# The end of a transformer block: last columns in two products, gate products in the gate's buffer, a quarter of the last x on TensorE

## The chip, the cores and the metric

The kernel runs on one core of one Trainium2 chip. The metric is the device time of one execution in microseconds (us), the median of three runs. A profiled execution, taken separately, gives the trace that is read below; its times are counted from the start of its span.

## The reference

One layer of a hybrid encoder block on an input x of 256 rows by 2048 columns, in float32. Three residual steps follow each other: a gated feed-forward network, a token-mixing step (chunked attention and a spatial gating unit side by side), and a second feed-forward network. Only the end of the third step matters here:

```python
h = modulate(rms_norm(x, ffn2_pre_g[l]), sh3, sc3)
y = swiglu(h, ffn2_w_gu[l], ffn2_w_down[l])
x = x + 0.5 * gt3 * rms_norm(y, ffn2_post_g[l])
```

`y` is 256 x 2048. `rms_norm` divides each row by the root of its mean square and multiplies by a gain for each column. So the last step needs, for each row, the sum of the squares of all 2048 columns of `y` before a single column of the output can be formed.

## The kernel before

The 256 rows are two tiles of 128 partitions, `t` = 0 and 1. The 2048 output columns are four blocks of `CH` = 512, `n` = 0 to 3. All big products are made of three float32r products each (helper `mm3`, lines 135 to 137): both operands are split into a high and a low part, and high*high, high*low and low*high are added in PSUM. Operands are loaded, split by ScalarE and VectorE (line 178 and 179), and multiplied by TensorE.

The feed-forward function `ffn` walks over the 5504 hidden columns in 11 chunks; the last chunk has 384. Its down projection ends in `down_last`, which adds the last chunk's contribution for all 2048 columns, and in the second feed-forward network (where `ahead` is None, so `tail` is true) this is the end of the program:

- `mm(t, n)`: 9 products of 128 x 512 into one PSUM bank (three 128-row pieces of the chunk, three products each).
- `evac(t, n, ps)`: VectorE adds the bank to `y[t]` (line 600), ScalarE squares the block and sums it (helper `square`, line 194), and VectorE multiplies the block by the gate in place (line 326). `g[0]` is the gate, one row of 2048 spread over the 128 partitions; it holds 0.5 * gt3 * ffn2_post_g. After n = 3, `rstd` (lines 199 and 201) has VectorE add the partial sums into `ms` and GpSimd raise the result to the power -1/2: that is `r`, one number for each row.
- `finish(t, y, r)`, here `finish3`: for each block j, VectorE computes x = y * r + x (line 1204), and SyncE starts the transfer of that block, 256 KB, to the output (line 1205).

The blocks of t = 0 are evacuated as their products end; the products of t = 1 follow at once, and are evacuated behind them (`late`). The program is written in this order, but a scheduler in the tile framework sets each engine's order, under `tc.high_priority()`. Tiles are taken from pools in turn: `pmm` has 6 PSUM banks, `sm` holds small tiles, and the tags "xn" and "h32" name buffers of `sm` that earlier stages use too. `new_sums(tag, n)` returns a tile for n partial sums and one column with epsilon, which GpSimd sets.

Of the kernel before, what the change touches and what calls it, by code (L numbers as in the profile page):

```python
# [12 lines left out]
F32 = mybir.dt.float32  # L13
F32R = mybir.dt.float32r
AF = mybir.ActivationFunctionType
ALU = mybir.AluOpType
AX = mybir.AxisListType

P = 128
D = 2048  # L20
# [8 lines left out]
CH = 512  # L29
# [54 lines left out]
def block_kernel(ctx: ExitStack, tc: tile.TileContext, a: dict, out: bass.AP):  # L84
    nc = tc.nc
# [8 lines left out]
    sm = ctx.enter_context(tc.tile_pool(name="sm", bufs=4))  # L94
    pmm = ctx.enter_context(tc.tile_pool(name="pmm", bufs=6, space=PSUM))
# [4 lines left out]
    def nm(s):  # L100
        uid[0] += 1
        return f"{s}_{uid[0]}"
# [30 lines left out]
    def mm3(ps, st, mv, start, stop):  # L133
        (ah, al), (wh, wl) = st, mv
        nc.tensor.matmul(ps, ah, wh, start=start, stop=False)  # L135
        nc.tensor.matmul(ps, ah, wl, start=False, stop=False)  # L136
        nc.tensor.matmul(ps, al, wh, start=False, stop=stop)  # L137
# [10 lines left out]
    def after(inst, first):  # L148

        tc.add_manual_dep(inst.ins, first.ins.name, mybir.DependencyInfo(  # L150
            mybir.DependencyClass.NoSync, mybir.DependencyReason.DATA), reason="order")
# [35 lines left out]
    def new_sums(tag, n):  # L187

        sums = sm.tile([P, n + 1], F32, tag=tag, name=nm(tag), bufs=2)
        nc.gpsimd.memset(sums[:, n:n + 1], EPS)  # L190
        return sums

    def square(junk, v, sums, i, width):
        return nc.scalar.activation(junk, v, AF.Square, scale=width ** -0.5, accum_out=sums[:, i:i + 1])
# [134 lines left out]
    def new_ysq():  # L329
        return [new_sums("ysq", 4) for _ in range(NT)]  # L330
# [16 lines left out]
    def ffn(wgu, wdn, h, avp, ahp, plan, rate, gate_of, finish, lead=(), after_lead=(), ahead=None,  # L347
# [5 lines left out]
        ps_of, acc, act_of, stat = {}, {}, {}, {}  # L353
# [222 lines left out]
        def down_last(c, g):  # L576

            off, w = CHUNKS[c]
            nk = w // P
            ysq = new_ysq()  # L580
            blocks = []
            tail = ahead is None
            for i in range(nk):
                raw = load(wdn, D * off + i * P * 2048, 2048)
                tick()
                for q in range(2):
                    wh, wl = split(raw[:, q * 1024:(q + 1) * 1024])
                    blocks += [(wh[:, :CH], wl[:, :CH]), (wh[:, CH:], wl[:, CH:])]
            if not tail:
                ahead()  # L590

            def mm(t, n):
                ps = pmm.tile([P, CH], F32, tag="mm", name=nm("dn"))
                for k in range(nk):
                    mm3(ps, (stat[c][t][0][:, k, :], stat[c][t][1][:, k, :]), blocks[n * nk + k], k == 0, k == nk - 1)
                return ps

            def evac(t, n, ps):
                ns = slice(n * CH, (n + 1) * CH)
                nc.vector.tensor_tensor(y[t][:, ns], y[t][:, ns], ps, op=ALU.add)  # L600
                return y_done(t, n, y, ysq, g, avp.tile([P, CH], F32, tag="av", name=nm("junk"), bufs=2))

            with tc.high_priority():
                for n in range(4):
                    r = evac(0, n, mm(0, n))
                late = [mm(1, n) for n in range(4)]
                if not tail:
                    finish(0, y, r)
                for n in range(4):
                    r1 = evac(1, n, late[n])  # L610
                if tail:
                    finish(0, y, r)
                finish(1, y, r1)

        todo, ready = [], []
        if plan:
# [561 lines left out]
    with ExitStack() as ahs:  # L1178
        avp = ahs.enter_context(tc.tile_pool(name="av2", bufs=2))
        gp = ahs.enter_context(tc.tile_pool(name="gp3", bufs=1))  # L1180
        prs = ExitStack()
        pre3 = prs.enter_context(tc.tile_pool(name="pre3", bufs=2))
        ahp = Lazy(tc, ahs, "ah2", 2, prs.close)
        use_slots((wx3, 3), (pre3, 2), (adap, 2), (wsp, 4))
        raw = sp3[2][0]
        lead = [sl for _, sls in sp3 for sl in sls] + [split(raw[:, 1024:])]

        def sum_tiles(t):

            flush_ada(GT[2])  # L1190
            pools = (((xp, "x0"), (xp, "x1")), ((const, "c_bc"), (gp, "gate")))[t]
            return [p.tile([P, KT, P], F32R, tag=tag, name=nm("ahl")) for p, tag in pools]

        x3 = []

        def gate3():
            flush_ada(GT[2])
            x3.extend(load_x(x2_dram, nc.gpsimd))
            return gate(2, 0.5, gp)

        def finish3(t, y, r):
            for j in range(4):
                js = slice(j * CH, (j + 1) * CH)
                nc.vector.scalar_tensor_tensor(out=x3[t][:, js], in0=y[t][:, js], scalar=r, in1=x3[t][:, js], op0=ALU.mult, op1=ALU.add)
                nc.sync.dma_start(out[t * P:(t + 1) * P, js], x3[t][:, js])

        ffn(a["w_gu2"], a["w_dn2"], h3, avp, ahp, None, 0.77, gate3, finish3, lead=lead,
            after_lead=((wx3, 3), (wsp, 4)), fast=FAST, sum_tiles=sum_tiles)

# [79 lines left out]
```

## Time and profile before

| | |
|---|---|
| median of 3 runs | 1825.6 us (1825.59 to 1826.73) |
| profiled execution, its own time | 1825.13 us |
| its span, first to last instruction | 1823.4 us |
| granted TensorE clock, mean | 0.996 |
| TensorE busy with products | 1789.1 us, 98% of the span |
| VectorE busy | 1455.0 us, 80% |
| ScalarE busy | 902.0 us, 49% |
| GpSimd busy | 33.5 us, 2% |

The span is shorter than the execution's own time by 1.73 us, which lie around it. PE is TensorE, PEld its loads of the stationary operand, DVE VectorE, ACT ScalarE, POOL GpSimd, SP SyncE; a q behind the name is the engine's queue or sequencer. A row of the chain of waits gives a start, a length and what was going on; a row of the timeline gives a start, the length of one or several instructions, the engine, the line and the tiles. A row of a table by windows gives the busy time of each engine in that stretch, the clock that TensorE was granted, the mean busy share of the 16 DMA engines and the rate in GB/s. Engines overlap one instruction's end with the next one's start, so the distance between starts can be less than the length of one.

### The profile page before, as it was taken

What the parts mean: (1) busy time and instruction counts of PE and PEld (TensorE: products, weight loads), DVE (VectorE), ACT (ScalarE), POOL (GpSimd) and SP (SyncE); (2) the same over time, 40 slices, a digit from 0 to 9 for tenths busy, and PEclk for the clock granted to TensorE, in tenths of its full rate; (3) what the DMA queues carried; (4) which work ended last, traced back from release to release, by engine and by line L of the source; (5) the groups of instructions that cost most, each with busy time, mean ns of one, the idle gap of its engine ahead of it and who ended that gap; (6) DMA issues with size and microseconds to landing.
All of it is one profiled execution on the core that took longest, in us unless ns stands there. A gap on an engine that the chain in (4) does not pass through costs nothing.

```text
span 1823.4 us, 21523 instructions
## 1 busy us (share of the span) xinstructions
PE 1789.1 (98%) x8199; PEld 1487.7 (82%) x8199; DVE 1455.0 (80%) x1659; ACT 902.0 (49%) x1166; POOL 33.5 (2%) x63
## 2 busy tenths in 40 slices
PE   7999999999999999999999999999999999999997
PEld 6777788888888898788888887888888888888886
DVE  6989997988778876858789987787447788788766
ACT  6544355444343335745555557445445455565552
POOL 0000000000000000000001100000000000000000
PEclk9999999999999999999999999999999999999999
DMA  9988788898888886469788985876556676676771
GB/s 394 390 329 315 284 320 344 328 366 332 337 327 330 319 331 240 182 242 361 286 333 329 348 349 203 317 300 250 196 188 231 214 285 240 222 266 247 257 254 69
DMA packets 75511, 522.19 MB, mean 286 GB/s; under 512 B 8416, under 2 KB 8592, under 8 KB 16656
## 3 DMA queue, kind: packets, MB, share of 16 engines
q1 hardware_dynamic: 74016, 511.36, 74.3%
q0 software_dynamic: 1296, 9.44, 1.2%
q8 instruction: 64, 1.05, 0.2%
q14 instruction: 39, 0.32, 0.1%
q10 hardware_dynamic: 96, 0.02, 0.0%
HBM read 514.47 MB, written 6.32 MB: 286 GB/s over the span
## 4 chain that ended last, share of the span: by engine, by line
PE 92%; DVE 3%; issue 3%; ACT 1%; DMA 0%; POOL 0%; POOLq 0%; DVEq 0%; SPq 0%; ACTq 0%
PE gu L137 14%; PE gu L136 14%; PE gu L135 14%; PE dn L135 8%; PE dn L136 8%; PE dn L137 8%; PE pj L135 4%; PE pj L137 4%; PE pj L136 4%; PE m L137 2%; PE m L136 2%; PE m L135 2%; PE wo L135 1%; PE wo L137 1%; PE wo L136 1%
## 5 line engine op out<-in xcount | busy, mean ns | idle before, releaser
L178 ACT CAST hi<-raw 128x1024 fp32r<-128x1024 f32 (+2 forms) x676 | 685.3, 1028 | 743.2 <-PE gu L137 301.9
L179 DVE TENSOR_TENSOR lo<-raw,hi 128x1024 fp32r<-128x1024 f32 (+2 forms) x676 | 788.1, 1190 | 205.5 <-ACT hi L178 202.5
L135 PE MATMUL gu<-hi,hhi 128*128 128x512 f32 (+1 forms) x1204 | 461.9, 387 | 8.8 <-DVE acc L417 4.2
L136 PE MATMUL gu<-lo,hhi 128*128 128x512 f32 (+1 forms) x1204 | 463.4, 385 | 0.4 <-DVE lo L179 0.3
L137 PE MATMUL gu<-hi,hlo 128*128 128x512 f32 (+1 forms) x1204 | 463.3, 385 | 0.0
L225 DVE CUSTOM_DVE_ANT_0 ada<-ada,c_bc,small 128x2048 f32<-128x2048 f32 x144 | 337.6, 2346 | 10.2 <-PE qkt L939 9.0
L135 PEld LDWEIGHTS gu<-hi,hhi 128*128 128x128 f32 x1204 | 226.1, 188 | 54.9 <-ACT hi L178 5.2
L136 PEld LDWEIGHTS gu<-lo,hhi 128*128 128x128 f32 x1204 | 227.1, 189 | 43.3 <-DVE lo L179 1.2
L137 PEld LDWEIGHTS gu<-hi,hlo 128*128 128x128 f32 x1204 | 226.9, 188 | 42.6
L135 PE MATMUL dn<-hi,ah 128*128 128x512 f32 x640 | 249.2, 389 | 0.0
L136 PE MATMUL dn<-lo,ah 128*128 128x512 f32 x640 | 249.1, 389 | 0.0
L137 PE MATMUL dn<-hi,al 128*128 128x512 f32 x640 | 249.1, 389 | 0.0
L135 PEld LDWEIGHTS dn<-hi,ah 128*128 128x128 f32 x640 | 120.1, 188 | 25.3
L136 PEld LDWEIGHTS dn<-lo,ah 128*128 128x128 f32 x640 | 120.1, 188 | 25.2
L137 PEld LDWEIGHTS dn<-hi,al 128*128 128x128 f32 x640 | 120.1, 188 | 25.0
L135 PE MATMUL pj<-hi,hhi 128*128 128x512 f32 x304 | 120.8, 397 | 0.0
L136 PE MATMUL pj<-lo,hhi 128*128 128x512 f32 x304 | 120.5, 396 | 0.0
L137 PE MATMUL pj<-hi,hlo 128*128 128x512 f32 x304 | 120.0, 395 | 0.0
L474 DVE TENSOR_TENSOR raw<-raw 128x512 f32<-128x512 f32 x96 | 66.2, 690 | 33.7 <-DMA raw<-in_w_gu_dram 32.4
L137 PEld LDWEIGHTS pj<-hi,hlo 128*128 128x128 f32 x304 | 57.1, 188 | 11.1
L135 PEld LDWEIGHTS pj<-hi,hhi 128*128 128x128 f32 x304 | 57.4, 189 | 10.6
L136 PEld LDWEIGHTS pj<-lo,hhi 128*128 128x128 f32 x304 | 57.4, 189 | 10.6
(199 smaller groups left out, 1450.3 us busy)
## 6 DMA issues: line engine op xcount, KB each, us to landing
raw<-in_w_gu_dram SPq DMA_DIRECT2D x158, 1024.0 KB, 4.9
ada<-in_w_ada_dram SPq DMA_DIRECT2D x144, 1024.0 KB, 6.9
raw<-in_w_dn_dram SPq DMA_DIRECT2D x86, 1024.0 KB, 5.0
raw<-in_w_in_dram SPq DMA_DIRECT2D x40, 1024.0 KB, 6.2
raw<-in_w_gu_dram SPq DMA_DIRECT2D x40, 768.0 KB, 4.8
raw<-in_w_out_dram SPq DMA_DIRECT2D x16, 1024.0 KB, 7.4
x<-x POOLq DMA_DIRECT2D x6, 1024.0 KB, 7.5
x<-in_x_dram SPq DMA_DIRECT2D x4, 1024.0 KB, 7.5
```

Of the source, the lines that this page charges most:

```text
L135: nc.tensor.matmul(ps, ah, wh, start=start, stop=False)
L136: nc.tensor.matmul(ps, ah, wl, start=False, stop=False)
L137: nc.tensor.matmul(ps, al, wh, start=False, stop=stop)
L178: i_hi = nc.scalar.copy(hi[:, :n], raw)
L179: i_lo = nc.vector.tensor_tensor(lo[:, :n], raw, hi[:, :n].bitcast(F32), op=ALU.subtract)
L225: inst = nc.vector.tensor_tensor_reduce(out=st, in0=st, in1=c_bc, scale=1.0, scalar=bada[:, i:i + 1], op0=ALU.mult, op1=ALU.add, accum_out ...
L474: nc.vector.tensor_tensor(blk[i], blk[i], blk[j], op=ALU.add)
```

## The change

In the tail of the second feed-forward network, for t = 1 alone:

1. The last 512 columns (n = 3) are computed as two products of 256 columns, each into a bank of its own, and are evacuated as two halves. There are then five partial sums of squares instead of four (a tile with the tag "ysq5").
2. The product with the gate is written over the gate, `g[0]`, instead of over `y[1]`. An explicit order puts the first half's gate product behind the second half's evacuation.
3. `finish3` for t = 1 forms the block j = 0 elsewhere: TensorE adds x (a product with the identity) and y * r (a product with a diagonal matrix `dg` of r, which ScalarE makes) in one PSUM bank, ScalarE copies the bank to a tile `xo` and starts its transfer from its own queue. VectorE forms the blocks 1 to 3 as before.

```diff
@@ down_last
             off, w = CHUNKS[c]
             nk = w // P
-            ysq = new_ysq()
+            tail = ahead is None
+            ysq = [new_sums("ysq", 4), new_sums("ysq5", 5) if tail else new_sums("ysq", 4)]
             blocks = []
-            tail = ahead is None
...
-            def mm(t, n):
-                ps = pmm.tile([P, CH], F32, tag="mm", name=nm("dn"))
+            def mm(t, n, cols=slice(0, CH)):
+                ps = pmm.tile([P, CH], F32, tag="mm", name=nm("dn"))[:, :cols.stop - cols.start]
                 for k in range(nk):
-                    mm3(ps, (stat[c][t][0][:, k, :], stat[c][t][1][:, k, :]), blocks[n * nk + k], k == 0, k == nk - 1)
+                    mm3(ps, (stat[c][t][0][:, k, :], stat[c][t][1][:, k, :]),
+                        [v[:, cols] for v in blocks[n * nk + k]], k == 0, k == nk - 1)
                 return ps
+
+            def evac_tail(late):
+
+                last = None
+                for i, (a, b, ps) in enumerate(late):
+                    inst = nc.vector.tensor_tensor(y[1][:, a:b], y[1][:, a:b], ps, op=ALU.add)
+                    if last:
+                        after(last, inst)
+                    square(avp.tile([P, CH], F32, tag="av", name=nm("junk"), bufs=2)[:, :b - a], y[1][:, a:b], ysq[1], i, D)
+                    prod = nc.vector.tensor_tensor(g[0][:, a:b], y[1][:, a:b], g[0][:, a:b], op=ALU.mult)
+                    last = prod if i == 3 else None
+                return rstd(ysq[1])
...
             with tc.high_priority():
                 for n in range(4):
                     r = evac(0, n, mm(0, n))
-                late = [mm(1, n) for n in range(4)]
-                if not tail:
+                if tail:
+                    hc = CH // 2
+                    late = [(n * CH, (n + 1) * CH, mm(1, n)) for n in range(3)]
+                    late += [(a, a + hc, mm(1, 3, slice(a - 3 * CH, a - 3 * CH + hc))) for a in (3 * CH, 3 * CH + hc)]
+                    r1 = evac_tail(late)
                     finish(0, y, r)
-                for n in range(4):
-                    r1 = evac(1, n, late[n])
-                if tail:
+                    finish(1, {1: g[0]}, r1)
+                else:
+                    late = [mm(1, n) for n in range(4)]
                     finish(0, y, r)
-                finish(1, y, r1)
+                    for n in range(4):
+                        r1 = evac(1, n, late[n])
+                    finish(1, y, r1)
@@ finish3
         def finish3(t, y, r):
-            for j in range(4):
+            if t:
+
+                js = slice(0, CH)
+                ps = pmm.tile([P, CH], F32, tag="mm", name=nm("xo"))
+                nc.tensor.matmul(ps, ident, x3[t][:, js], start=True, stop=False)
+                dg = sm.tile([P, P], F32, tag="h32", name=nm("dg"), bufs=2)
+                nc.scalar.mul(dg, ident, r)
+                nc.tensor.matmul(ps, dg, y[t][:, js], start=False, stop=True)
+                xo = sm.tile([P, CH], F32, tag="xn", name=nm("xo"), bufs=2)
+                nc.scalar.copy(xo, ps)
+                nc.scalar.dma_start(out[t * P:(t + 1) * P, js], xo)
+            for j in range(t, 4):
                 js = slice(j * CH, (j + 1) * CH)
```

The order of the instructions on the engines, apart from line numbers, is the same in both programs up to the last block of t = 1; a GpSimd instruction that sets one column of a sums tile also stands earlier, at the start of the program.

VectorE at the program's end, before. The tiles: `y_1872` and `x_2629` belong to t = 0, `y_1873` and `x_2630` to t = 1, `dn_14038`, `dn_14048` and `dn_14058` are the banks of t = 1 for n = 1, 2 and 3, `r_14025` and `r_14085` are r of t = 0 and 1:

```order
L600 TENSOR_TENSOR y_1873_9725<-y_1873_9725,dn_14038 128x512
L1204 SCALAR_TENSOR_TENSOR x_2629_13616<-y_1872_9724,r_14025,x_2629_13616 128x512
L600 TENSOR_TENSOR y_1873_9725<-y_1873_9725,dn_14048 128x512
L326 TENSOR_TENSOR y_1873_9725<-y_1873_9725,gate_13666 128x512
L1204 SCALAR_TENSOR_TENSOR x_2629_13616<-y_1872_9724,r_14025,x_2629_13616 128x512
L326 TENSOR_TENSOR y_1873_9725<-y_1873_9725,gate_13666 128x512
L600 TENSOR_TENSOR y_1873_9725<-y_1873_9725,dn_14058 128x512
L199 TENSOR_REDUCE ms_14083<-ysq_13936 128x1
L326 TENSOR_TENSOR y_1873_9725<-y_1873_9725,gate_13666 128x512
L1204 SCALAR_TENSOR_TENSOR x_2630_13617<-y_1873_9725,r_14085,x_2630_13617 128x512 x4
```

VectorE at the same place now (line 603 is the evacuation, 607 the gate product, 1233 the output; `dn_14058` and `dn_14068` are the two halves):

```order
L603 TENSOR_TENSOR y_1873_9725<-y_1873_9725,dn_14048 128x512
L1233 SCALAR_TENSOR_TENSOR x_2629_13616<-y_1872_9724,r_14025,x_2629_13616 128x512
L607 TENSOR_TENSOR gate_13666<-y_1873_9725,gate_13666 128x512
L603 TENSOR_TENSOR y_1873_9725<-y_1873_9725,dn_14058 128x256
L603 TENSOR_TENSOR y_1873_9725<-y_1873_9725,dn_14068 128x256
L607 TENSOR_TENSOR gate_13666<-y_1873_9725,gate_13666 128x256 x2
L199 TENSOR_REDUCE ms_14098<-ysq_2691_13936 128x1
L1233 SCALAR_TENSOR_TENSOR x_2629_13616<-y_1872_9724,r_14025,x_2629_13616 128x512
L1233 SCALAR_TENSOR_TENSOR x_2630_13617<-gate_13666,r_14100,x_2630_13617 128x512 x3
```

The fourth output block of t = 0 (`x_2629`) stood two instructions ahead of the last evacuation, and now stands behind `ms`; the last gate product stood behind `ms`, and now stands, as two halves, ahead of it; the output of t = 1 has three instructions instead of four.

TensorE's last rows, before:

```order
L135 MATMUL dn_14058<-hi_13964,aw_13930 128x512
L136 MATMUL dn_14058<-lo_13965,aw_13930 128x512
L137 MATMUL dn_14058<-hi_13964,aw_13931 128x512
L135 MATMUL dn_14058<-hi_13964,aw_13930 128x512
L136 MATMUL dn_14058<-lo_13965,aw_13930 128x512
L137 MATMUL dn_14058<-hi_13964,aw_13931 128x512
```

And now:

```order
L136 MATMUL dn_14068<-lo_13965,aw_13930 128x256
L137 MATMUL dn_14068<-hi_13964,aw_13931 128x256
L135 MATMUL dn_14068<-hi_13964,aw_13930 128x256
L136 MATMUL dn_14068<-lo_13965,aw_13930 128x256
L137 MATMUL dn_14068<-hi_13964,aw_13931 128x256
L1224 MATMUL xo_14110<-x_2630_13617,ident 128x512
L1227 MATMUL xo_14110<-gate_13666,dg_14112 128x512
```

Nine products of 512 columns have become eighteen of 256, and two of plain float32 stand behind them.

ScalarE's last rows, before:

```order
L194 ACTIVATE junk_14021,ysq_13934<-y_1872_9724 128x512
L194 ACTIVATE junk_14069,ysq_13936<-y_1873_9725 128x512
L194 ACTIVATE junk_14073,ysq_13936<-y_1873_9725 128x512
L194 ACTIVATE junk_14077,ysq_13936<-y_1873_9725 128x512
L194 ACTIVATE junk_14081,ysq_13936<-y_1873_9725 128x512
```

And now:

```order
L194 ACTIVATE junk_14087,ysq_2691_13936<-y_1873_9725 128x512
L194 ACTIVATE junk_14091,ysq_2691_13936<-y_1873_9725 128x256
L194 ACTIVATE junk_14095,ysq_2691_13936<-y_1873_9725 128x256
L1226 ACTIVATE dg_14112<-ident,r_14100 128x128
L1229 COPY xo_14115<-xo_14110 128x512
L1230 DMA out_dram<-xo_14115 128x512
```

The last square is two, and three instructions follow that wait for r.

## The prediction

> **What bounds the kernel now.** First the head of the page.
>
> ```profile
> span 1823.4 us, 21523 instructions
> PE 1789.1 (98%) x8199; PEld 1487.7 (82%) x8199; DVE 1455.0 (80%) x1659; ACT 902.0 (49%) x1166; POOL 33.5 (2%) x63
> ```
>
> TensorE carries nearly the whole span, and the change takes no work from it there: up to the last block of t = 1 each engine has the same order as before. What it can move is the stretch behind the last products. I read it in the chain that ended last, in order of time (start, length, what).
>
> ```profile
> 1807.68 0.68 DVE y L600
> ...
> 1812.75 0.66 DVE x L1204
> 1813.41 0.60 DVE y L326
> 1814.01 0.61 DVE y L600
> ...
> 1814.70 0.63 ACT junk L194
> ...
> 1815.46 0.17 DVE ms L199
> ...
> 1816.66 0.75 DVE x L1204
> 1817.41 0.66 DVEq L1285
> 1818.07 1.32 DVE x L1204 x2
> ```
>
> From 1807.68 to 1814.62 VectorE is busy without a gap: four evacuations and three gate products of t = 1 at 0.60 each, and the four output blocks of t = 0 at 0.66. Then comes a relay: 0.76 from the start of the last square to `ms`, 1.20 from `ms` to the first output block of t = 1, while r is made, and then four output blocks, the last done at 1818.07 + 1.32 = 1819.39. The span still runs 4.0 us from there, so I look at the transfers: the output's issues, and the windows behind them (the last two numbers are the share of the 16 DMA engines and GB/s; the one ahead of them is TensorE's granted clock).
>
> ```profile
> L1205 SPq DMA_DIRECT2D out_dram<-x x8: 332/332/343, 1809.0 to 1819.4; - x8
> DMA to landing us min/median/max: 2.4/2.6/2.9
> 1814.20:1815.00 0.80, 0.00 (x0) 0.00 (x0) 0.41 (x1) 0.29 (x1) 0.00 (x0) 1.00 0.84 328
> 1817.80:1818.20 0.40, 0.00 (x0) 0.00 (x0) 0.40 (x2) 0.00 (x0) 0.00 (x0) 0.64 0.00 0
> 1818.20:1819.00 0.80, 0.00 (x0) 0.00 (x0) 0.80 (x2) 0.00 (x0) 0.00 (x0) 0.50 0.89 346
> 1819.00:1820.00 1.00, 0.00 (x0) 0.00 (x0) 0.39 (x1) 0.00 (x0) 0.00 (x0) 0.50 1.11 336
> 1820.00:1821.00 1.00, 0.00 (x0) 0.00 (x0) 0.00 (x0) 0.00 (x0) 0.00 (x0) 0.50 1.07 326
> 1821.00:1821.60 0.60, 0.00 (x0) 0.00 (x0) 0.00 (x0) 0.00 (x0) 0.00 (x0) 0.50 0.53 184
> ```
>
> The reader is to see two things. A transfer alone (the last of t = 0, 1814.2 to 1815.0) costs 0.80 * 0.84 = 0.67 us of all 16 engines; the four of t = 1 cost 0.71 + 1.11 + 1.07 + 0.32 = 3.21 us, 0.80 each, and they flow without a gap from about 1818.25 to 1821.5. The first starts 0.84 us behind the end of its block (1817.41). The last block, done at 1819.39, would alone have flowed from 1820.23 to 1820.9; it ended 0.6 later. So the end is not set by VectorE's fourth block but by when the *first* block of t = 1 is ready, plus 3.21 us in which the DMA engines are full, plus 1.9 us of landing and closing.
>
> **The change part by part.** *The halves on TensorE.* The products of t = 1, n = 3, and a place where 256-column products run:
>
> ```profile
> 1810.98 0.39 PE L135 MATMUL dn<-hi,aw 128*128 128x512 f32 x1
> ...
> 1812.79 0.39 PE L137 MATMUL dn<-hi,aw 128*128 128x512 f32 x1
> 854.33 0.28 PE L135 MATMUL sp<-kz,qt 128*128 128x256 f32 x1
> 854.33 0.19 PEld L136 LDWEIGHTS sp<-kz,qt 128*128 128x128 f32 x1
> 854.44 0.28 PE L136 MATMUL sp<-kz,qt 128*128 128x256 f32 x1
> 854.45 0.19 PEld L137 LDWEIGHTS sp<-kz,qt 128*128 128x128 f32 x1
> 854.56 0.28 PE L137 MATMUL sp<-kz,qt 128*128 128x256 f32 x1
> ```
>
> Nine products of 512 take (1812.79 - 1810.98) / 8 = 0.226 each. At 256 columns starts are 0.115 apart, though each has its own load of 0.19: loads run under products, two deep. Eighteen halves then start up to 1810.98 + 17 * 0.115 = 1812.94 and end at 1813.22, as the nine do. This is the term with the thinnest evidence, three products in a row. Its upper end is a half that costs as much as a whole, 0.226 (a rival below); the lower end is 0.113, half a whole.
>
> *VectorE.* Ahead of the last evacuation there now stand three evacuations, three gate products and three output blocks of t = 0, from 1807.68: 3 * (0.60 + 0.66 + 0.60) = 5.58, to 1813.26. For half blocks I take the difference of two forms of one line, on each engine:
>
> ```profile
> L292 DVE TENSOR_TENSOR hlo<-h,hhi 128x512 fp32r<-128x512 f32 x16 | 11.0, 691 | 5.6 <-ACT hhi L291 5.6
> L292 DVE TENSOR_TENSOR hlo<-h,hhi 128x256 fp32r<-128x256 f32 x16 | 6.7, 420 | 0.0
> L291 ACT CAST hhi<-h 128x512 fp32r<-128x512 f32 x16 | 10.0, 622 | 0.2
> L291 ACT CAST hhi<-h 128x256 fp32r<-128x256 f32 x16 | 6.5, 407 | 0.5
> ```
>
> A half saves VectorE 0.27 and ScalarE 0.215. So the halves start at 1813.26 and 1813.59 (0.60 - 0.27 = 0.33 apart; the second bank was full at 1813.22) and are done at 1813.68 and 1814.01. The gate products of the halves follow to 1814.6, beside the squares. ScalarE's first half square starts 0.09 behind its evacuation (as 1814.70 behind 1814.61), 1813.77, and holds ScalarE for 0.73 - 0.215 = 0.515; the second starts at 1814.29, and `ms` 0.76 - 0.215 = 0.545 later, at 1814.83 instead of 1815.46: **-0.63**. Of this, 0.66 is the output block of t = 0 that now waits behind `ms`, given back in part (0.07) by the split's extra instruction; the squares give 0.04. The moved block (0.75) runs from about 1814.9 to 1815.65, inside the 1.20 in which r is made, so it costs nothing; if r came sooner it would stand in the way of the first block of t = 1. Its transfer, a queue place ahead of those of t = 1, flows from 1816.5 to 1817.2, before they need the engines.
>
> *The gate's buffer.* In place, a gate product must wait until the square has read `y`. On t = 1 VectorE had no gap for that (the chain above), so the new target is worth nothing by itself; it lets the half products run while the squares do.
>
> *The quarter on TensorE.* VectorE's output falls from four blocks to three, 0.66 less. The other path is ScalarE's diagonal, a product, a copy, an issue:
>
> ```profile
> L977 ACT ACTIVATE sb<-sb,mx 128x128 f32<-128x128 f32 x16 | 6.3, 393 | 1.2 <-DVE mx L973 1.2
> L413 ACT COPY acc<-gu 128x512 f32<-128x512 f32 x20 | 11.4, 590 | 10.2 <-PE gu L137 9.9
> 1015.50 1.95 PE L1064 MATMUL zp<-uv,wst 128*128 128x128 f32 x16
> gd<-grow ACTq DMA_DIRECT2D x3, 8.0 KB, 4.0
> ```
>
> The program asks for 16 plain float32 products of `zp` and the trace has 32 records, so one is two records; 16 records in 1.95 us make 0.22 for 128 columns, and at most 4 * 0.22 + 0.17 = 1.06 for 512 (0.62 if a record of 512 costs as one of float32r, 0.226). The product with x waits for nothing and runs under the squares, by 1814.3. From r at 1816.03 (1814.83 + 1.20): diagonal 0.39, product 0.19 + 0.62 to 1.06, copy 0.59, 0.1 of handing over, so the issue comes at 1817.9 to 1818.4; I take the later, since the nearest row is the plain float32 one. VectorE's third block is done at 1816.03 + 0.75 + 2 * 0.66 = 1818.10. Both paths end some 1.0 to 1.3 sooner than 1819.39.
>
> But the transfers are what counts. First block 1816.78, flow from 1817.62, 3.21 us of full engines, to 1820.83 instead of 1821.46: **the 0.66 saved on VectorE is covered by the drain, and only the 0.63 of `ms` is left**. The fourth transfer is in time if it starts by 1817.62 + 3 * 0.80 = 1820.0, and at 1818.4 + 0.84 it does. Whether a second queue moves more than 336 GB/s no row shows. [...]
>
> *The rest.* One more GpSimd set of a column at the start stands beside the wait for the first loads, and costs nothing.
>
> **Sum.** 1823.4 - 0.63 = 1822.8 of span; with the 1.73 around it 1824.5 against the profiled 1825.13. The median of the runs, 1825.6, is 0.47 above the profiled one, so the forecast is 1825.6 - 0.63 = 1825.0. 0.2% of 1825.6 is 3.65 us, about what can be told from no change: the whole relay from 1814.6 to the last block is 4.8 us long, so I expect no change that can be told.
>
> **The rivals.** *No drain.* If each transfer cost 0.67 as one alone, the last block would set the end: 1819.39 - 1818.1 = 1.29 sooner, 1824.3. For it: alone they are cheaper. Against: engines full for 3.2 us.
>
> *A half costs a whole (slower).* At 0.226 each, the last half starts at 1810.98 + 17 * 0.226 = 1814.82, ends at 1815.1, its evacuation at 1815.55, and `ms` stands at 1816.2: +0.7, 1826.3. It decides from a distance of 0.184 on (second evacuation at 1814.40). For it: the load's 0.19 lies just there. Against: 0.115 in `sp`.
>
> *Loads don't run under products.* A half would cost 0.19 + 0.115 = 0.30, the last start would be 1816.1, `ms` 1817.5: +2.0, 1827.6. Against: loads of 0.19 start 0.12 apart. [...]
>
> *The fourth block lands late.* ScalarE's queue took 4.0 us to land 8 KB, beside full loads. An issue at 1818.4 would land at 1822.4, against 1819.4 + 2.9 = 1822.3 before: 1825.7, nothing gained. A cold clock for the diagonal product would add to this: TensorE's clock fell at about 1817.9, 4.7 us behind its last product; now the gap is from 1814.3 to 1816.5, 2.2 us, so I don't expect it.
>
> **How the numbers follow.** Forecast 55%; no drain 15%; fourth block late or the gain of `ms` otherwise lost (1825.7) 17%; a half costs a whole 7%; loads not hidden 2%; something elsewhere by more than 3.65 us, 4%. All but the last lie within 0.2%. Range: from 1824.3 to 1826.3 by the cases, widened by the scatter of the runs (1825.59 to 1826.73, and 1825.13 profiled), 1823.8 to 1826.8. Faster by over 0.2%: 2%; within: 96%; slower: 2%.
>
> **What would show it.** Right: 256-column products 0.115 apart; `ms` 7.15 us behind the first evacuation of t = 1 instead of 7.78; the moved block between `ms` and r; DMA engines full for about 3.2 us from 0.84 behind VectorE's first block; the last square's half alone between evacuation and `ms`. Wrong: a gap on VectorE ahead of the second half's evacuation; the transfers over in clearly less than 3.2 us, with the end set by the last block; a transfer of ScalarE's that flows alone at the end.

## The result, and the profile after

The changed kernel takes 1841.8 us (median of 4 runs, 1839.96 to 1843.69), the kernel before 1825.6 beside it: a ratio of 1.0087, 95% interval 1.0072 to 1.0102. It is slower by 16 us, and not the 0.6 faster of the forecast. The profiled execution took 1841.94 us.

First the head of the page after, whose span is 16.7 us longer.

```profile
span 1840.1 us, 21556 instructions
PE 1810.9 (98%) x8212; PEld 1489.9 (81%) x8212; DVE 1456.0 (79%) x1660; ACT 901.7 (49%) x1170; POOL 33.6 (2%) x63
```

VectorE, ScalarE and GpSimd are busy as long as before, within 1 us. TensorE is busy 21.8 us longer (1789.1 before) with only 13 records more: nine from the halves, and four of the two plain float32 products, which take 3.0 us in all. Where the rest begins is seen by windows, first the kernel before, then the kernel after. The columns are the window, its length, and the busy time of PE, PEld, DVE, ACT and POOL, each with its count.

```profile
0.00:250.00 250.00, 234.63 (x1007) 190.35 (x1008) 217.96 (x247) 119.81 (x158) 2.36 (x19) 0.99 0.87 341
250.00:500.00 250.00, 250.00 (x1131) 207.29 (x1131) 214.88 (x216) 114.89 (x128) 0.00 (x0) 1.00 0.88 340
```

```profile
0.00:250.00 250.00, 234.99 (x1012) 190.80 (x1013) 218.63 (x247) 120.52 (x158) 2.39 (x20) 0.99 0.87 341
250.00:500.00 250.00, 250.00 (x1112) 204.01 (x1111) 210.90 (x213) 110.43 (x124) 0.00 (x0) 1.00 0.87 338
```

Up to 250 us the two keep step. From 250 to 500 both have TensorE busy without a gap at a clock of 1.00, and the kernel after starts 1112 products where the kernel before starts 1131. So a product itself takes longer there, and for no wait. The same products one by one, from the timeline by line; before, then after:

```profile
300.65 0.39 PE L135 MATMUL dn<-hi,ah 128*128 128x512 f32 x1
...
302.01 0.39 PE L135 MATMUL dn<-hi,ah 128*128 128x512 f32 x1
```

```profile
300.81 0.40 PE L137 MATMUL dn<-hi,al 128*128 128x512 f32 x1
...
301.98 0.39 PE L136 MATMUL dn<-lo,ah 128*128 128x512 f32 x1
```

Six starts in 1.36 us before, 0.227 each; five in 1.17 after, 0.234 each. These are among the first down projections of the first feed-forward network, 1500 us ahead of the tail that the change is about.

The tail itself came out nearly as forecast. VectorE, GpSimd, ScalarE's queue, and two of the 18 half products with the two products of `xo`:

```profile
1825.03 0.68 DVE L603 TENSOR_TENSOR y<-y,dn 128x512 f32<-128x512 f32 x1
...
1830.62 0.74 DVE L603 TENSOR_TENSOR y<-y,dn 128x256 f32<-128x256 f32 x2
...
1832.06 0.16 DVE L199 TENSOR_REDUCE ms<-ysq 128x1 f32<-128x6 f32 x1
1832.14 0.74 DVE L1233 SCALAR_TENSOR_TENSOR x<-y,r,x 128x512 f32<-128x512 f32 x1
1833.32 2.07 DVE L1233 SCALAR_TENSOR_TENSOR x<-gate,r,x 128x512 f32<-128x512 f32 x3 [0.44 <-POOL r L201]
1832.37 0.92 POOL L201 TENSOR_TENSOR r<-ms,mhalf 128x1 f32<-128x1 f32 x1 [6.83 <-DVE ms L199]
1836.42 0.39 ACTq L1230 DMA_DIRECT2D out_dram<-xo  x1
1828.48 0.28 PE L135 MATMUL dn<-hi,aw 128*128 128x256 f32 x1
...
1830.52 0.28 PE L137 MATMUL dn<-hi,aw 128*128 128x256 f32 x1
1830.64 1.02 PE L1224 MATMUL xo<-x,ident 128*128 128x512 f32 x2
1833.78 1.99 PE L1227 MATMUL xo<-gate,dg 128*128 128x512 f32 x2 [2.12 <-ACT dg L1226]
```

From the first evacuation of t = 1, `ms` is 7.03 us away (7.78 before, 7.15 forecast), and the end of the span 1840.1 - 1825.03 = 15.07 (1823.4 - 1807.68 = 15.72 before): -0.65. The transfers, in the windows behind (the last two columns are the share of the DMA engines and GB/s):

```profile
1834.80:1835.20 0.40, 0.40 (x2) 0.00 (x0) 0.40 (x1) 0.00 (x0) 0.00 (x0) 0.50 0.65 256
1835.20:1836.00 0.80, 0.56 (x1) 0.00 (x0) 0.20 (x1) 0.20 (x1) 0.00 (x0) 0.50 1.06 374
1836.00:1837.00 1.00, 0.00 (x0) 0.00 (x0) 0.00 (x0) 0.39 (x1) 0.00 (x0) 0.50 1.04 309
1837.00:1838.00 1.00, 0.00 (x0) 0.00 (x0) 0.00 (x0) 0.00 (x0) 0.00 (x0) 0.50 0.88 305
1838.00:1838.40 0.40, 0.00 (x0) 0.00 (x0) 0.00 (x0) 0.00 (x0) 0.00 (x0) 0.50 0.26 82
```

0.26 + 0.85 + 1.04 + 0.88 + 0.10 = 3.13 us of full engines for the four blocks of t = 1, against 3.21 before. So -0.65 in the tail, and, with the span 16.7 us longer, about +17.3 ahead of it.

### The profile page after: what moved, and what is told of

Same layout as the page of the kernel before. It is cut to its first block, busy times and chain, and to the rows that moved or that the text cites. A ratio compares the mean times of both kernels' runs of the same rounds, so it can differ in the third digit from the quotient of the medians.

```text
span 1840.1 us, 21556 instructions
## 1 busy us (share of the span) xinstructions
PE 1810.9 (98%) x8212; PEld 1489.9 (81%) x8212; DVE 1456.0 (79%) x1660; ACT 901.7 (49%) x1170; POOL 33.6 (2%) x63
## 3 DMA queue, kind: packets, MB, share of 16 engines
q8 instruction: 64, 1.05, 0.2%
## 4 chain that ended last, share of the span: by engine, by line
PE 92%; DVE 3%; issue 2%; ACT 2%; DMA 1%; POOL 0%; POOLq 0%; SPq 0%; DVEq 0%; ACTq 0%
PE gu L135 14%; PE gu L137 14%; PE gu L136 14%; PE dn L135 8%; PE dn L136 8%; PE dn L137 8%; PE pj L137 4%; PE pj L135 4%; PE pj L136 4%; PE m L137 2%; PE m L135 2%; PE m L136 2%; PE wo L135 1%; PE wo L137 1%; PE wo L136 1%
## 5 line engine op out<-in xcount | busy, mean ns | idle before, releaser
L135 PEld LDWEIGHTS gu<-hi,hhi 128*128 128x128 f32 x1204 | 226.5, 188 | 55.7 <-ACT hi L178 5.2
L136 PEld LDWEIGHTS gu<-lo,hhi 128*128 128x128 f32 x1204 | 227.1, 189 | 44.6 <-DVE lo L179 1.2
L137 PEld LDWEIGHTS gu<-hi,hlo 128*128 128x128 f32 x1204 | 226.9, 188 | 44.7
```

## What the experiments compare

The order of instructions up to the tail is the same, so something else about the products must differ. The tag "ysq5" is new in the pool `sm`: two buffers of 24 bytes in each partition, 32 each as placed, 64 together. In the built program every pool behind `sm` (the operands `ah` and `al`, some of the buffers of the split weights `hi` and `lo`, `x`, `av`, the gate, and others) starts 64 bytes later than before; `hhi`, `hlo`, the first four buffers each of `hi` and `lo`, and whatever else lies in front of `sm` have stayed. So of many products one operand moved and the other did not. In a row such as `dn<-hi,ah` the first operand, `hi`, is streamed through TensorE, and the second, `ah`, is the stationary, which PEld loads ahead (before, a load of `ah` starts at 1774.87 and takes 0.19, and its product starts at 1775.09). The theory became: a product of 512 columns in float32r is slower when the streamed operand and the stationary loaded for the next product start at different places, counted modulo some power of two (the start as a byte address in a partition).

Each trace gives the start of every product, and the program gives its operands' addresses; the two lists match one to one. Products are grouped by the start of the streamed operand and the start of the next product's stationary, modulo 256 bytes. The tables below give the mean distance to the next start, in ns, with the number of products. Distances above 260 ns, 2% of them, are left out. Such a distance can't be read off a single row of the page.

```
moved by:                  0 (before)     64 (after)
both at 0                  227.3  x6956   228.1  x3157
stationary moved alone         -          233.2  x1788
streamed moved alone           -          230.3  x1212
both moved                     -          227.9  x794
96 stationaries at 224     234.0  x96     232.8, 235.4  x64, x32
sum of all distances, us   1603.3 x7052   1619.5 x7047
```

The means are 227.35 and 229.81, so 7050 products make 2.46 * 7050 ns = 17.3 us, and 17.3 - 0.65 is the 16.7 by which the spans differ. Note the 96 slow ones that the kernel before already had: stationaries `ahl` in the buffer of `c_bc`, which starts at 224.

The grouping by the *next* stationary is a choice that these traces don't force, since nearly every product's own stationary lies at the same place as the next one. Where they differ, products are slow either way: before, 234.4 (x48) with only the next stationary at 224, and 232.9 (x48) with only the product's own there; after, 230.3 (x74) with only the next one 64 bytes behind the streamed operand's place, and 232.9 (x38) with only the product's own there.

## Experiments

**The change without the new buffer.** The five sums are put under the old tag, whose buffer has room for them. Nothing else differs from the change, and no buffer moves against the kernel before.

```diff
-ysq = [new_sums("ysq", 4), new_sums("ysq5", 5) if tail else new_sums("ysq", 4)]
+ysq = [new_sums("ysq", 4), new_sums("ysq", 5 if tail else 4)]
```

> The changed kernel with one word different: the five partial sums take the tag ysq instead of a tag ysq5 of their own. Their tile is no larger than the slot that the tag has, so no tile moves in SBUF against the kernel before; the tail is the changed one. Address theory (the new tag pushed every pool behind it by 64 bytes, and TensorE's products are slower where the operand that streams and the operand that is being loaded lie differently modulo 128 bytes): 1825.0 us, products of 512 columns 0.2267 apart nearly everywhere as before, the tail 0.65 shorter than before. Tail theory (the sixteen us come from what the change does at the end, or from the program being longer): 1841 to 1842 us.

Measured 1825.01 us (10 runs, 1823.67 to 1826.2) against 1825.2: 0.9997, interval 0.9988 to 1.0006. Distances are back at 227.3 (x6950). The 16 us hang on the tag. From the profile (the last row is from the chain of waits):

```profile
1806.84 0.68 DVE L603 TENSOR_TENSOR y<-y,dn 128x512 f32<-128x512 f32 x1
...
1813.87 0.16 DVE L199 TENSOR_REDUCE ms<-ysq 128x1 f32<-128x6 f32 x1
...
1815.13 2.08 DVE L1233 SCALAR_TENSOR_TENSOR x<-gate,r,x 128x512 f32<-128x512 f32 x3 [0.44 <-POOL r L201]
1815.59 1.14 PE xo L1227 x2
```

The span ends at 1821.9, 15.06 behind the first evacuation, as in the changed kernel; but the diagonal product takes 1.14 here, at a granted clock of 1.00, and 1.99 there, at 0.50. Its cold clock costs nothing at the end there.

**128 bytes, and the move without the change.** One kernel adds an unused 64 bytes behind `sm` to the changed kernel, so that the later pools are moved by 128. Another adds them to the kernel before, and does nothing of the change. A third puts them into the kernel before ahead of nearly all tiles, so that nearly all move by 64 together.

```diff
+padp = ctx.enter_context(tc.tile_pool(name="padp", bufs=1))
+pad = padp.tile([P, 16], F32, tag="pad", name="pad")
+nc.gpsimd.memset(pad, 0.0)
```

The third takes the same tile from the pool `const`, behind its last tile and ahead of nearly all other pools:

```diff
+pad = const.tile([P, 16], F32, tag="pad", name="pad")
+nc.gpsimd.memset(pad, 0.0)
```

> The changed kernel as it is, with 64 bytes per partition more behind the small tiles, so that the tiles behind them are moved by 128 instead of 64 bytes. Address theory, modulo 128: 1825.0 us, as with no move. If any move costs, or if the distance counts modulo 256: 1841 us. Tail theory: 1841 to 1842 us.

> The kernel before, with 64 unused bytes per partition behind the small tiles and nothing else. Address theory: 1842 us, that is the changed kernel's 1841.8 and the 0.65 that its tail saves; products with the one operand moved and the other not 230 to 233 ns apart. Tail theory: 1825.6 us.

> The kernel before, with 64 unused bytes ahead of nearly all tiles: both operands of nearly all big products then lie 64 bytes past a multiple of 128. If only the difference of the two operands counts: 1825.6 us, within 1.5. If each address counts by itself (a start that is no multiple of 128 costs): every one of 7055 products of 512 columns is 3 to 7 ns slower, 1847 to 1875 us. Tail theory: 1825.6 us.

```
                           128 (after)    64 (before)    64, all (before)
us, median                 1843.21        1841.98        1825.0
ratio to before            1.0099         1.0090         0.9997
 95% interval              1.0084-1.0114  1.0075-1.0105  0.9987-1.0006
both at 0                  227.8  x3161   228.1  x3170       -
stationary moved alone     232.7  x1790   233.2  x1788       -
streamed moved alone       232.7  x1212   230.3  x1212       -
both moved                 228.0  x793    227.9  x794    227.3  x6958
```

The kernel before with 64 idle bytes is as slow as the change. Moving nearly everything together costs nothing, so it is the difference of the two starts that counts. A move by 128 did not heal it: the modulus isn't 128, and the expectation that it was is refuted.

**Products alone.** A program with products only, in series of 48 that differ in where the two operands start; nothing else runs on the core beside them. In a series all stationaries start at the same place modulo 256. Its line of the product:

```diff
+nc.tensor.matmul(ps[:, :cols], s[:, k:k + 128], m[:, j:j + cols], start=i == 0, stop=i == n - 1)
```

> Only products, and nothing of the block: groups of 48 products with the streamed operand and the loaded operand starting at 0, 32, 64, 96 (and 128, 192) bytes past a multiple of 128; the output is a copy of x. Its time says nothing. Address theory by difference: 227 ns at equal starts and at a distance of 128, 230 to 235 where they differ by 32, 64 or 96, with nothing else running on the core. If the slowdown needs other engines or DMA at SBUF: 227 everywhere. Halves of 256 columns: 115 at equal starts, 120 at a distance of 64 (as the changed kernel's halves ran at the end). bfloat16 is a guess: the same sign.

```
512 columns, float32r: stationary less streamed, modulo 256
   0      32     64     96     128    192    224
 226.7  233.4  233.4  234.4  232.5  228.9  233.2    ns from start to start
256 columns, float32r:  0: 119.8    64 and -64: 117.8
512 columns, bfloat16:  215.8 at every place
```

Equal starts at 32, 64 or 96 also give 226.7, and every pair of places agrees with its difference to 0.2 ns. No other engine takes part. A distance of 128, which was expected to be free, takes 232.5. The loads themselves last as long in every float32r series of 512 columns, 187 to 188 ns; it is the products that start further apart. The sign matters: -64 (192) costs 2.2 ns and +64 costs 6.7. At 256 columns the effect is reversed, where 115 and 120 had been expected, and bfloat16, of which the same sign had been guessed, doesn't show it.

**A move by 192.** If the sign matters, this swaps the two groups of the move by 64.

```diff
+pad = padp.tile([P, 48], F32, tag="pad", name="pad")
+nc.gpsimd.memset(pad, 0.0)
```

> The kernel before with an unused tile of 192 bytes a partition behind the pool of small tiles: every later pool is moved by 192 bytes. Theory (what counts is the stationary's start less the streamed operand's, modulo 256, and -64 costs 2.2 ns a product where +64 costs 6.7): 1788 products now have -64, 1212 have +64, so 1788 * 2.2 + 1212 * 6.7 = 3.9 + 8.1 = 12.0 us, the time 1837.2, ratio 1.0066 +/- 0.0015, less than the 1842.0 of the move by 64. Rival (only whether the two differ counts, or the distance without its sign): as the move by 64, 1842 or more, ratio 1.009.

Measured 1838.19 us, ratio 1.0071 (1.0058 to 1.0085), 13.0 us and not 16.8 as for 64. The stationary moved alone has 229.4 (x1789), the streamed operand moved alone 233.2 (x1212). The direction counts, as the products alone said.

**Finer places, and one odd stationary in sixteen.**

> Products of 128 x 128 by 512 columns in float32r alone, nothing beside them (the output is a copy of x, its time says nothing): series of 48 whose stationaries begin 0, 4, 8, 16, 24, 48, 80, 112, 144, 160, 176, 208, 232, 240, 248 and 252 bytes ahead of the streamed operand modulo 256; one series with one and the same stationary; one with the stationaries moved by 256; 384, 256 and 128 columns at 0 and at 32; and three series of 128 in which every sixteenth stationary begins at 224, 32 or 64. Theory (start distance set by the difference modulo 256): 0 and the move by 256 at 226.7 ns, most differences at 232 to 234, small ones like 4 and 252 also slow if only the exact place counts, and 226.7 if it is a matter of a coarser grain (16 or 32 bytes). In the series with one odd stationary in sixteen, theory A (only the product during which the odd one is loaded) has 1 of 16 at 233 and a mean of 227.1; theory B (as in the kernel, the products behind it are slow too) has several at 228 to 233 and a mean of 228 to 230. At 256 columns equal places 119.8, at 32 some 117.8 as at 64; at 384 and 128 nothing is known.

```
stationary less streamed, modulo 256, 512 columns, ns
   4      8      16     24     48     80     112    144
 232.4  230.7  233.3  231.1  233.3  232.0  233.3  233.4
  160    176    208    232    240    248    252    256
 233.2  230.0  233.3  231.1  228.4  233.3  226.7  226.8
one odd stationary in sixteen: the product in which it is loaded, and the next three
 at 224: 235.0  232.0  227.0  226.0     at 32: 235.0  228.3  232.6  230.7
 at 64:  226.0  235.7  228.4  232.6, then 230.7; all others 226.0 to 227.0
columns 384: 173.3 equal, 173.3 at 32    256: 119.9, 118.3    128: 111.7, 111.7
```

(The 173.3 for 384 columns at equal places leaves out the first eight products, some of which are slower.) Four bytes are enough (232.4), and a move by the full 256 costs nothing (226.8); it isn't a matter of a coarser grain. But 252, which is four bytes the other way, is as fast as equal places (226.7), against the expectation: equality is enough for the best pace, and not needed for it. Between, the price follows no simple line (228.4 at 240, 233.3 at 248).

One odd stationary costs about 14 ns at 224 and 20 at 32 and 64, over two to four products: theory B in kind, though fewer products than in the kernel, and with means of 227.5 to 227.8 below the forecast 228 to 230. At 64 the product in which the odd one is loaded is not slow (226.0), and the product that uses it is (235.7); at 224 and 32 the former is slow already (235.0). So whether a product's own stationary or the next one counts stays open, and may depend on the distance. Where all stationaries of a stretch lie alike it makes no difference.

**A better version.** The 96 `ahl` stationaries at 224 are in the kernel before too. With the sums under the old tag, `mhalf` is reserved ahead of `c_bc`, which then starts at 0; no byte is added.

```diff
+    mhalf = const.tile([P, 1], F32, tag="mhalf", name="mhalf")
     c_bc = const.tile([P, D], F32, tag="c_bc", name="c_bc")
...
-    mhalf = const.tile([P, 1], F32, tag="mhalf", name="mhalf")
```

> The changed kernel with its five sums under the old tag (no buffer moves), and in addition the 4-byte constant mhalf is reserved ahead of c_bc instead of behind ident. No byte is added; c_bc, ident and the 96 stationaries that lie behind ident now begin at 0 instead of 224 modulo 256 bytes. Theory (a 512-column float32r product is slower when the operand being streamed and the operand being loaded next begin at different places modulo 256 bytes): the 96 products that stood at 234.0 ns from start to start fall to 227.3, 0.64 us in all, so 1825.0 becomes 1824.4, ratio to the kernel before about 0.9993 less 0.0002, 0.9993 +/- 0.001. Rival (only the big pools matter, or the slow 96 are slow because of the form of their work): they stay at 234 and the time at 1825.0.

Measured 1822.74 us (11 runs, 1821.26 to 1824.82): 0.9988 of the kernel before, interval 0.9979 to 0.9997. It has the lowest median of all that ran. All products now start from equal places (227.1, x7051).

```profile
span 1819.5 us, 21556 instructions
PE 1785.7 (98%) x8212; PEld 1485.1 (82%) x8212; DVE 1452.6 (80%) x1660; ACT 902.5 (50%) x1170; POOL 34.2 (2%) x63
```

The gain over the same change without this (1825.01) is more than the 0.64 expected. The mean distance over all products fell from 227.36 to 227.10, 1.8 us on 7050. In the kernel without it, the products that follow a product with an odd next stationary stood at 232.8, 233.6, 224.8, 229.8, 233.2, 227.9, 231.1 and 229.7, and only those behind them at 226.9; the same eight stand at 226.5 to 227.3 here. So the price of the 96 had been read from 96 products alone, while the products behind them pay too. What remains of the 2.3 us lies within the scatter of the runs, and part of that scatter is TensorE's clock: over the 123 runs of the kernel before and of the six variants within 0.2% of it, a mean granted clock lower by 0.001 goes with 0.5 us more. A straight line fitted through them puts the change under the old tag 0.8 us (+/- 0.3, one standard error) below the kernel before at equal clock, and this version another 1.6 (+/- 0.3) below that, near the 0.65 and 1.8 read from the traces.

**The tail: without the quarter on TensorE.** The sums are under the old tag, and VectorE forms all four blocks of t = 1.

```diff
-            if t:
...
-            for j in range(t, 4):
+            for j in range(4):
```

> The changed kernel with its five sums under the old tag, and without the quarter on TensorE: VectorE forms all four blocks of t = 1 and SyncE starts their transfers. Theory (the 0.66 us that VectorE saves are covered by the four transfers, 3.2 us of full DMA engines): from the first evacuation of t = 1 to the end of the span 15.06 us as with the quarter, within 0.15, and the time within 0.2 us of 1825.0. Rival (no drain, VectorE's last block sets the end): 15.06 + 0.66 = 15.7 us, 1825.7. Either way ms stands 7.03 behind the first evacuation.

```profile
1809.30 0.68 DVE L603 TENSOR_TENSOR y<-y,dn 128x512 f32<-128x512 f32 x1
...
1816.33 0.16 DVE L199 TENSOR_REDUCE ms<-ysq 128x1 f32<-128x6 f32 x1
...
1817.59 2.74 DVE L1222 SCALAR_TENSOR_TENSOR x<-gate,r,x 128x512 f32<-128x512 f32 x4 [0.44 <-POOL r L201]
```

1824.46 us (10 runs), 0.9996 (0.9987 to 1.0005). The span of 1824.3 ends 15.0 behind the first evacuation, 15.06 with the quarter. VectorE's last block is done 0.66 later and the end doesn't move: the transfers cover it, as forecast, and the quarter on TensorE is worth nothing that these runs can tell.

**The tail: a whole last block.** The last block of t = 1 is one product, one evacuation and one square again; the quarter and the gate's buffer stay.

```diff
-ysq = [new_sums("ysq", 4), new_sums("ysq5", 5) if tail else new_sums("ysq", 4)]
+ysq = [new_sums("ysq", 4), new_sums("ysq", 4)]
...
-late = [(n * CH, (n + 1) * CH, mm(1, n)) for n in range(3)]
-late += [(a, a + hc, mm(1, 3, slice(a - 3 * CH, a - 3 * CH + hc))) for a in (3 * CH, 3 * CH + hc)]
+late = [(n * CH, (n + 1) * CH, mm(1, n)) for n in range(4)]
```

> The changed kernel with its five sums' tag as before, and the last block of t = 1 whole: one product of 512 columns, one evacuation, four sums. The quarter on TensorE and the gate's buffer stay. The scheduler then puts all four output blocks of t = 0 ahead of ms again. Theory (ms came sooner because one output block of t = 0 went behind it, not because of the halves' shorter work): VectorE works without a gap from the first evacuation, 4 * (0.60 + 0.66 + 0.60) = 7.44 us, so ms stands 7.4 to 7.55 behind the first evacuation instead of 7.03, the span's end 15.4 to 15.6 behind it instead of 15.06, and the time is 1825.4. Rival (the square of the last block sets ms, as before): 7.03 to 7.1, nothing lost; a second rival, that the halves' finer steps saved a full evacuation and square: 7.8 as in the kernel before, 15.7 to the end.

```profile
1807.81 0.68 DVE L603 TENSOR_TENSOR y<-y,dn 128x512 f32<-128x512 f32 x1
...
1815.27 0.14 DVE L199 TENSOR_REDUCE ms<-ysq 128x1 f32<-128x5 f32 x1
1816.13 2.08 DVE L1231 SCALAR_TENSOR_TENSOR x<-gate,r,x 128x512 f32<-128x512 f32 x3 [0.72 <-POOL r L201]
1815.55 0.55 POOL L201 TENSOR_TENSOR r<-ms,mhalf 128x1 f32<-128x1 f32 x1 [7.24 <-DVE ms L199]
1818.70 0.58 ACT L1227 COPY xo<-xo 128x512 f32<-128x512 f32 x1 [2.17 <-PE xo L1225]
```

1824.95 us, 0.9998 (0.9989 to 1.0008). `ms` stands at 7.46, as expected. But the first block of t = 1 follows it by 0.86 and not by 1.26, and comes 8.32 behind the first evacuation, as good as the 8.29 with halves. GpSimd's power took 0.55 us where VectorE was idle, and 0.92 in the changed kernel, where the moved block runs beside it. The span ends 1823.1 - 1807.81 = 15.29 behind the first evacuation, a little sooner than the 15.4 to 15.6 expected. The 0.2 over 15.06 is put down to the late copy on ScalarE (1818.70), behind a cold diagonal product of 2.09: ScalarE's transfer is issued at 1819.32, and the share of the DMA engines falls from 0.99 in the window of 1 us from 1819 to 0.82 in the one from 1820.

In the kernel before the same power took 0.86, beside the last gate product:

```profile
1815.54 0.68 DVE L326 TENSOR_TENSOR y<-y,gate 128x512 f32<-128x512 f32 x1
1815.76 0.86 POOL L201 TENSOR_TENSOR r<-ms,mhalf 128x1 f32<-128x1 f32 x1 [7.58 <-DVE ms L199]
```

**The tail: the power alone.** If the power is slowed by VectorE, nothing should stand beside it. On top of the better version, TensorE and ScalarE form the last block of t = 0 instead of the first of t = 1.

```diff
-            if t:
-                js = slice(0, CH)
+            if not t:
+                js = slice(3 * CH, D)
...
-            for j in range(t, 4):
+            for j in range(3 + t):
```

> The kernel of e6_even_ident (sums under the old tag, mhalf ahead of c_bc), but TensorE, ScalarE and ScalarE's queue form the last block of t = 0 (columns 1536 to 2047) instead of the first of t = 1; VectorE forms three blocks of t = 0 and all four of t = 1. Nothing of VectorE's then stands between ms and the first output block of t = 1. Theory (GpSimd's power takes 0.55 us while VectorE is idle and 0.86 to 0.92 while VectorE works beside it, as seen with the whole last block): ms 7.03 behind the first evacuation as now, the power 0.55, the first output block 0.86 behind ms instead of 1.26, the end 6.7 behind that, so 14.6 us from the first evacuation to the end instead of 15.06, and 1822.3 us against 1822.7. Rival (the power was short by chance, or because ScalarE was idle): 0.92, 1.26 and 15.0, nothing gained. A loss is possible if ScalarE's transfer of t = 0 flows into those of t = 1: 15.3.

```profile
1805.50 0.68 DVE L603 TENSOR_TENSOR y<-y,dn 128x512 f32<-128x512 f32 x1
...
1812.53 0.16 DVE L199 TENSOR_REDUCE ms<-ysq 128x1 f32<-128x6 f32 x1
1813.42 2.74 DVE L1233 SCALAR_TENSOR_TENSOR x<-gate,r,x 128x512 f32<-128x512 f32 x4 [0.73 <-POOL r L201]
1812.84 0.55 POOL L201 TENSOR_TENSOR r<-ms,mhalf 128x1 f32<-128x1 f32 x1 [6.83 <-DVE ms L199]
1813.48 1.35 ACTq L1230 DMA_DIRECT2D out_dram<-xo  x1
1815.00:1816.00 1.00, 0.00 (x0) 0.00 (x0) 1.00 (x2) 0.00 (x0) 0.00 (x0) 1.00 1.03 377
1816.00:1817.00 1.00, 0.00 (x0) 0.00 (x0) 0.16 (x1) 0.00 (x0) 0.00 (x0) 0.52 1.14 227
1817.00:1818.00 1.00, 0.00 (x0) 0.00 (x0) 0.00 (x0) 0.00 (x0) 0.00 (x0) 0.50 1.05 289
1818.00:1819.00 1.00, 0.00 (x0) 0.00 (x0) 0.00 (x0) 0.00 (x0) 0.00 (x0) 0.50 1.03 340
1819.00:1820.00 1.00, 0.00 (x0) 0.00 (x0) 0.00 (x0) 0.00 (x0) 0.00 (x0) 0.50 0.21 78
```

The power took 0.55 and the first block came 7.92 behind the first evacuation, 0.37 sooner, as the theory has it. ScalarE ran its copy of `xo` beside it (0.59 from 1812.87), so an idle ScalarE was not what made the power short. The end came at 15.7, 0.6 later, and the time is 1823.85 us (0.9993, 0.9984 to 1.0002), no gain over the better version. ScalarE's issue at 1813.48 took 1.35 us, where that of the changed kernel took 0.39, and its transfer of t = 0 runs among those of t = 1: 1.03 + 1.14 + 1.05 + 1.03 + 0.21 = 4.46 us of full engines, five blocks instead of four. The loss named beforehand came true, and was larger than its 15.3: each block took 0.89 and not 0.80. Why is open.

## Why the prediction was wrong, point by point

- **The step that failed is the first: "What it can move is the stretch behind the last products"**, from the same order on each engine. The order was the same, but 64 bytes of a small pool moved one operand or both of more than half of the big products. The sum had the products of the body at no change, and they took 17.3 us more (229.81 ns from start to start in place of 227.35). The new tag, named in the diff, had no price in the sum; the one case that could hold it, "something elsewhere by more than 3.65 us, 4%", had neither a mechanism nor a place. The run with the old tag (1825.01) and the kernel before with 64 idle bytes (1841.98) show it from both sides. Why the places matter to TensorE stays open.
- A row for it stood in the trace of before: 96 products at 234 ns in place of 227, all with a stationary from one buffer at another place. The mean of a line doesn't show it; distances grouped by address do.
- **`ms` 0.63 sooner** was right in size, 0.75 measured; the first block of t = 1 is 0.69 sooner and the end 0.65. Its parts were not as forecast: the run with the whole block, with all four output blocks of t = 0 ahead of `ms`, has 7.46 where the kernel before has 7.78, so 0.32 comes without the moved block and the halves, and only 0.43 with both. The halves start 0.12 apart (0.115 forecast), so "a half costs a whole" doesn't hold here. Nor do the loads wait for the products: in the changed kernel those of the halves take 0.19 and start 0.12 apart, while products of 0.28 run.
- **The drain** was right: 3.13 us of full engines, and the run without the quarter ends as soon. The sum kept the 3.21 us of one queue for two, which no row of before shows; it was the author's estimate. In the runs the four blocks take 3.13 with two queues (the changed kernel) and 3.21 with one (the kernel before).
- **"The gate's buffer ... worth nothing by itself"** was wrong in its mechanism. With the whole block, quarter and new buffer, the first block comes 8.32 behind the first evacuation, where the kernel before needs 8.98: all four gate products now stand ahead of `ms`, and `r` is made with VectorE idle. The halves add 0.03. What the new buffer does with neither quarter nor halves wasn't run, nor was it parted from the new order in the program, where the sum for `ms` is written behind the last gate product and not ahead of it.
- **"The moved block ... costs nothing"** was wrong by about 0.4: it lengthens the power from 0.55 to 0.92. In the kernel before, the gate product behind `ms` did the same (0.86), so the difference from before is small (1.26 against 1.20).
- **"A cold clock ... I don't expect it"** was wrong in the changed kernel: the clock fell 2.2 us behind the product with x, and the diagonal product took 1.99. The drain covers it. Under the old tag the same product was warm (1.14).

## What to carry to other kernels

When a change adds or widens any buffer, even one of a few bytes, in a kernel of float32r products of 512 columns, compare the start addresses of all operands of the big products before and after, modulo 256; the same order of instructions is no proof of the same time (here 64 bytes cost 17.3 us of 1825.6). If products back to back run some per cent below their best pace at full clock and no row shows a wait, group the distances between starts by the addresses of the streamed operand and of the stationaries, the product's own and the next (here 227.3 ns with both at 0, and 233.2 with the stationary moved alone). And before work is taken off an engine at the end of a kernel, see whether the last transfers, and not that engine, set the end (here VectorE's last block came 0.66 us sooner, and the end stayed at 15.06 us behind the first evacuation, 15.0 without).

## What the runs showed of the hardware

- Float32r products of 512 columns alone, back to back: 226.7 ns when the streamed operand and the stationaries start at the same place modulo 256 bytes, and also with the stationaries at 252; 228.4 to 234.4 at the other differences tried. The effect is absent in bfloat16 (215.8) and reversed at 256 columns (119.8 against 117.8). The addresses of the two together set the pace: both at 32, 64 or 96 give 226.7 as both at 0 do, and a difference costs up to 7.7 ns. Why is open; the runs show only the dependence.
- GpSimd's power over 128 numbers, at the end of the program: 0.55 us with VectorE idle (the whole block, the power alone), 0.86 to 0.92 beside a VectorE instruction on two of the kernel's buffers (`y` and the gate before, `y` and `x` after). In both the power ends 0.4 us behind VectorE's instruction, after (1832.14 + 0.74 = 1832.88, and 1833.29) as before (1815.54 + 0.68 = 1816.22, and 1816.62). By what the one holds up the other, no run shows.
- TensorE's clock after the gap ahead of the diagonal product: warm after 2.28 us under the old tag (1.14 us for the pair), cold after 2.12 in the changed kernel (1.99) and after 2.40 with the whole block (2.09). So the gap alone doesn't decide. In the traces of before and after, the changes of the granted clock lie whole multiples of 3.413 us apart (before, for instance, 3.413, 30.72 and 692.9 us, which are 1, 9 and 203 of them). In the changed kernel and with the whole block the clock fell 2.2 us behind the product with x, and the 3.41 us ahead of the fall still held 1.2 us of products. What sets the fall is open.
